# One part of a hybrid encoder step: the gated SSD output kept in its gate's tile, and the Z stores moved to another queue

## The chip, the core and the metric

The program runs on one core of one Trainium2 chip. The metric is the device time of one execution in microseconds. Before the change three runs gave 1900.34, 1905.69 and 1907.13 us; their median is 1905.69 us.

The core has engines with queues of their own that work side by side: TensorE (PE in the profile, its weight loads PEld), VectorE (DVE), ScalarE (ACT), GpSimd (POOL) and SyncE (SP), which here only issues DMAs. An engine takes its instructions in the order of its queue, and an instruction that waits holds up all that stand behind it.

## What is computed

One layer of an encoder runs over 2048 prompt tokens and 64 sample tokens of width 1024, in float32. Cut to what matters here:

```python
h = rmsnorm(x, norm_g)
z_a, xbc, dt_raw, u_b, z_b = split(h @ w_in)
y = ssd_scan(...) + d_ssd[:, None] * xs           # SSD branch, chunk by chunk
y = y * silu(z_a)                                 # its gate
y_a = rmsnorm(y in 4 groups of 256 columns, ssd_norm_g)
y = gelu(S5 scan of u_b); y = y * sigmoid(y @ w_glu + b_glu)
y_b = y * silu(z_b)                               # the gate of the S5 branch
out = rmsnorm(x + concat(y_a, y_b) @ w_out, final_norm_g)
```

The change touches two places: the product `y * silu(z_a)` with its norm, and the store of `silu(z_b)`.

## The kernel before

The tokens are worked through in two stages, `st` 0 (the sample tokens and the first 1024 prompt tokens) and `st` 1 (the other 1024). Within a stage the SSD branch is cut into four groups `g` of four heads. For each group `phase_s_proj` (L746) computes the projections and `phase_s_chunks` (L840) runs the scan, over nine chunks of up to 128 tokens in stage 0 and eight in stage 1. Each matrix product of the projections is done as three matmuls on split halves (`hi`, `lo`) and summed in PSUM.

The gate. `gate()` (L752) projects `z_a` for one chunk after another into a PSUM tile `psz`, and ACT writes `silu(psz)` into a tile `zt` of tag `zs` (L765 to L777). The tag has nine buffers, as many as a group of stage 0 has chunks. The list `zs[c]` keeps them for the scan.

The scan. For each chunk `a1` (L849) transposes inputs on PE into `pA`; `a2` (L867) scales them; `b1` (L888) does the matmuls into `pY` and `pH`; `b2` (L915) updates the state `h` and forms the chunk's output; `b3` (L947) and `b4` (L956) do the norm and the store. The loop at L963 issues `b3`, `b1`, `a1`, then `b4`, `a2`, `b2`, for different chunks. Of the output's path:

```python
act.mul(out=y, in_=pY, mul=ea)                    # b2, L933, four heads
tt(y, y, xs_, ALU.add); tt(y, y, zs[c], ALU.mult) # b2, L935, L936
actf(zs[c], y, AF.Square, accum_out=rs)           # b3, L951, the squares themselves unused
act.mul(out=y, in_=y, mul=rs)                     # b4, L959
pool.dma_start(out=YA[...], in_=y)                # b4, L960
```

The tile `y` (L927) has the pool's two buffers. A buffer is given to the next tile of its tag when all that reads and writes the old one is done, a DMA's landing included; `reuse_waits="tile"` stands at each pool. The PSUM tiles `pA`, `pY`, `pH` and others share the four banks of the pool `sd` (L76); the projections have four banks of their own, the pool `pj` (L75). The norm needs POOL twice: L952 and L953 make the root from the sum `rs`.

The other branch. `phase_uz_block` (L342) projects two blocks of 128 rows of `u_b` or `z_b` into `psu`. ACT copies them (L363) or puts them through Silu (L365) into a tile `ub` (L351) of the pool `big`, seven buffers. POOL then stores U in eight DMAs (L371) or Z in one (L374) per block of 128 rows; there are 16 Z stores in all. Z is read much later, by SP (L1013), into `zt` of `phase_g`.

The order. Generators are woven by hand in the lines from L1306 on: the projections of the S5 branch run as the main thread, with the scan's steps, the preparation of the S5 tables (`PREP`; `prep_mats` L469 and `prep_tabs` L555, mostly on DVE) and in stage 1 the S5 scan (`s5_steps` L663) let in between. That is the order in which the program is written. The builder then sets the order on each engine from a time plan of its own; for ACT and DVE in `phase_g` the written order is kept (`tc.manual_schedule`, L1401 and L1414). In the trace L60 is `tt`, L57 `stt`, L66 `actf`, L69 `mm` and L212 the copy in `split`.

Of the kernel before, what the change touches and what calls it, by code (L numbers as in the profile page):

```python
# [12 lines left out]
AF = mybir.ActivationFunctionType  # L13
ALU = mybir.AluOpType
# [29 lines left out]
def tile_hybrid_stream(  # L44
# [8 lines left out]
    act, dve, pool, sp = nc.scalar, nc.vector, nc.gpsimd, nc.sync  # L53
# [5 lines left out]
    def tt(out, a, b, op):  # L59
        dve.tensor_tensor(out=out, in0=a, in1=b, op=op)  # L60
# [4 lines left out]
    def actf(out, in_, func, **kw):  # L65
        nc.scalar.activation(out=out, in_=in_, func=func, **kw)  # L66
# [12 lines left out]
    Z = dram.tile([8, D, KT], F32, name="Z")  # L79
# [135 lines left out]
    def wblock(segs):  # L215
        his, los = [], []
        n = sum(s[1] for s in segs)
        for kh in range(2):
            raw = rawp.tile([128, 4, 272], F32, tag="raw", name="raw")
            o = 0  # L220
            for c0, w in segs:
                sp.dma_start(out=raw[:, :, o:o + w],
                             in_=w_in[0, kh * 512:(kh + 1) * 512, c0:c0 + w].rearrange("(k p) c -> p k c", p=128))
                o += w
            hi = wp.tile([128, 4, 272], F32R, tag="whi", name="whi")
            lo = wp.tile([128, 4, 272], F32R, tag="wlo", name="wlo")
            split(hi[:, :, :n], lo[:, :, :n], raw[:, :, :n])
            his.append(hi)
            los.append(lo)
        return his, los  # L230

    def proj_cm(ps, W, m0, piece):

        hi, lo, _ = piece
        for k in range(8):
            wh = W[0][k // 4][:, k % 4, m0:m0 + 128]
            wl = W[1][k // 4][:, k % 4, m0:m0 + 128]
            mm(ps, wh, hi[:, k], k == 0, False)
            mm(ps, wh, lo[:, k], False, False)
            mm(ps, wl, hi[:, k], False, k == 7)  # L240
# [95 lines left out]
    def kcols(st):  # L336

        if st == 0:
            return [(0, 0, 64, 0), (0, 64, 256, 9), (1, 0, 384, 41), (2, 0, 384, 89)], 137, 0
        return [(0, 0, 256, 0), (1, 0, 384, 32), (2, 0, 384, 80)], 129, 137  # L340

    def phase_uz_block(st, pcs, blk, kind):  # L342
        runs, K, c0 = kcols(st)
        W = wblock([((C_U if kind == "u" else C_ZB) + 256 * blk, 256)])
        piece_outer = st == 0 and blk == 3 and kind == "z"
        ubs, ths = {}, {}
        order = [(m, i) for i in range(3) for m in range(2)] if piece_outer else [(m, i) for m in range(2) for i in range(3)]
        for m, i in order:
            b = 2 * blk + m
            if i == 0:  # L350
                ubs[m] = big.tile([128, 8, 137], F32, tag="big", name="ub")  # L351
                pool.memset(ubs[m][:, :, 8:9] if st == 0 else ubs[m][:, :, 128:129], 0.0)
            ub = ubs[m]
            ps = pj.tile([128, 512], F32, tag="pj", name="psu")
            proj_cm(ps[:, :PIECES[st][i]], W, 128 * m, pcs[i])
            for (pi, off, n, k0) in runs:
                if pi != i:
                    continue
                nk = n // 8
                src = ps[:, off:off + n].rearrange("p (k s) -> p s k", s=8)  # L360
                dst = ub[:, :, k0:k0 + nk]
                if kind == "u":
                    act.copy(out=dst, in_=src)  # L363
                else:
                    actf(dst, src, AF.Silu)  # L365
            if i < 2:
                yield
                continue
            if kind == "u":
                for j in range(8):  # L370
                    pool.dma_start(out=U[8 * b + j, :, :, c0:c0 + K].rearrange("s c k -> c s k"),  # L371
                                   in_=ub[16 * j:16 * j + 16, :, :K])
            else:
                pool.dma_start(out=Z[:, 128 * b:128 * b + 128, c0:c0 + K].rearrange("s c k -> c s k"), in_=ub[:, :, :K])  # L374
            yield


# [462 lines left out]
    def phase_s_chunks(st, g, p, SS, V):  # L840
# [3 lines left out]
        zs, x0, x1, Bc, Cc = V[g]  # L844

        hsl = slice(4 * g, 4 * g + 4)
        live = {}
# [67 lines left out]
        def b2(c):  # L915

            n, pi, off, cc, ro = chs[c]
            hst, pY, pH, xs_ = live[c]
            sample = st == 0 and c == 0
            zero = st == 0 and c == 1  # L920
            if zero:
                act.copy(out=hst, in_=pH[:, :256])
            else:
                tt(hst.rearrange("p (h q) -> p h q", h=4), hst.rearrange("p (h q) -> p h q", h=4),
                   dec[:, c, hsl].unsqueeze(2).to_broadcast([128, 4, 64]), ALU.mult)
                tt(hst, hst, pH[:, :256], ALU.add)
            y = p.tile([128, 256], F32, tag="y", name="y")  # L927
            tt(xs_[:n], xs_[:n], pY[:n, 0:256], ALU.add)
            if zero:
                tt(y[:n], xs_[:n], zs[c][:n], ALU.mult)  # L930
            else:
                for h in range(4):
                    act.mul(out=y[:n, 64 * h:64 * h + 64], in_=pY[:n, 256 + 64 * h:320 + 64 * h],  # L933
                            mul=ea[:n, c, 4 * g + h:4 * g + h + 1])
                tt(y[:n], y[:n], xs_[:n], ALU.add)  # L935
                tt(y[:n], y[:n], zs[c][:n], ALU.mult)  # L936
            if sample or (c == NC - 1 and st == 1):
                dst = (o_ssd_s if sample else o_ssd_p)[0, 0].rearrange("h p n -> (h p) n")
                pst = sd.tile([128, 512], F32, tag="sd", name="pso")
                for j in range(2):  # L940
                    nc.tensor.transpose(pst[:, 128 * j:128 * j + 128], hst[:, 128 * j:128 * j + 128], ident)
                ho = big.tile([128, 2, 128], F32, tag="big", name="ho")
                act.copy(out=ho, in_=pst[:, :256].rearrange("p (j n) -> p j n", j=2))
                pool.dma_start(out=dst[256 * g:256 * g + 256].rearrange("(j q) n -> q j n", q=128), in_=ho)
            live[c] = y

        def b3(c):  # L947
            n = chs[c][0]
            y = live[c]
            rs = p.tile([128, 1], F32, tag="rs2", name="rs2", bufs=4)  # L950
            actf(zs[c][:n], y[:n], AF.Square, scale=1.0 / 16, accum_out=rs[:n])  # L951
            pool.tensor_scalar(out=rs[:n], in0=rs[:n], scalar1=1.0, scalar2=EPS, op0=ALU.mult, op1=ALU.add)  # L952
            pool.tensor_tensor(out=rs[:n], in0=rs[:n], in1=mhalf[:n], op=ALU.pow)  # L953
            live[c] = y, rs

        def b4(c):  # L956
            n, pi, off, cc, ro = chs[c]
            y, rs = live.pop(c)
            act.mul(out=y[:n], in_=y[:n], mul=rs[:n])  # L959
            pool.dma_start(out=YA[ro:ro + n, 256 * g:256 * g + 256], in_=y[:n])  # L960

# [359 lines left out]
    for b in range(4):  # L1321
        C = phase_s_chunks(0, b, spool, SS, V)
        if b == 0:
            pp = aux.enter_context(tc.tile_pool(name="pp", bufs=1, reuse_waits="tile"))
            P = []
            PP = prep_params(pp, P)
            weave(phase_uz_block(0, pcs, 0, "u"), (PP, 1.34), (C, RA))
            drain(PP)
            pw = aux.enter_context(tc.tile_pool(name="pw", bufs=1, reuse_waits="tile"))
            PREP = chain(*(chain(prep_mats(k, pw, P), prep_tabs(k, 0, pw, P), prep_tabs(k, 1, pw, P)) for k in range(4)))  # L1330
            weave(phase_uz_block(0, pcs, 0, "z"), (C, RA), (PREP, RP))
            drain(C)
            weave(phase_s_proj(0, pcs, 1, spool, SS, V), (PREP, RP))
        elif b < 3:
            weave(chain(phase_uz_block(0, pcs, b, "u"), phase_uz_block(0, pcs, b, "z")), (C, RA), (PREP, RP))
            drain(C)
            weave(phase_s_proj(0, pcs, b + 1, spool, SS, V), (PREP, RP))
        else:
            weave(phase_uz_block(0, pcs, 3, "u"), (C, RC), (PREP, RP))
            drain(PREP)  # L1340
# [110 lines left out]
```

## Time and profile before

| | |
|---|---|
| three runs, median | 1905.69 us (1900.34 to 1907.13) |
| the profiled execution, its own time | 1902.07 us |
| its span, from the first instruction to the last | 1900.3 us |
| mean granted clock of TensorE | 0.989 |
| busy: PE, PEld, DVE, ACT, POOL | 1831.1, 1709.4, 1096.5, 908.6, 378.3 us |
| DMA, mean rate over the span | 129 GB/s |

The scans and projections take the time to about 1366 us, with the work of `phase_g` from 1290 to 1507 us and the output projection after that. How to read the rows below: in a list of waits a line is the engine and source line that waited, what ended the wait, the total in us, the number of times and the longest. In a timeline a line is start, duration, engine, source line, operation, the tile written and the tiles read, the shapes, and a count of merged instructions; in brackets stands how long the engine sat idle before it and what ended that. An engine with a q behind it (ACTq) is its queue, seen at issuing a DMA.

### The profile page before, as it was taken

The page shows a single profiled execution, that of the slowest core. Times are in us where ns is not written, and L with a number is a line of the kernel's source. Part 1 is how long each engine was busy: PE and PEld are TensorE (multiplying, and loading weights), DVE is VectorE, ACT ScalarE, POOL GpSimd, SP SyncE. Part 2 cuts the span into 40 slices and gives each one's busy share as a digit, 9 for nine tenths or more (in the row PEclk, how much of TensorE's full clock was granted, in tenths as well). Part 3 has the DMA queues.
Part 4 walks back from the last instruction along what each step waited for, and adds up shares of the span by engine and source line. Part 5 has one row for each costly group of instructions (what it writes and reads, how often), then busy time and mean ns, then how long its engine had stood idle before and what let it go on. Part 6 is the DMA issues. An engine that isn't in the chain of part 4 may idle for free. (4 is left out here: it accounts for less than half of the span.)

```text
span 1900.3 us, 31061 instructions
## 1 busy us (share of the span) xinstructions
PE 1831.1 (96%) x11400; PEld 1709.4 (90%) x11400; DVE 1096.5 (58%) x2157; ACT 908.6 (48%) x2505; POOL 378.3 (20%) x730
## 2 busy tenths in 40 slices
PE   7998999999899899999999999999999999999998
PEld 6998999999899799889989999998999988887886
DVE  5688687685767653776678567857544432212221
ACT  5466465545646633666666556656544421111110
POOL 3022314233332411032013301212211000001000
PEclk9999999999999999999999999999999999999999
DMA  5224545454444454456545754536455553313220
GB/s 165 76 72 101 155 105 137 127 137 103 121 128 111 143 137 119 139 153 182 152 136 164 206 159 125 152 95 178 134 161 161 186 181 92 97 56 95 92 86 34
DMA packets 197816, 244.69 MB, mean 129 GB/s; under 512 B 41696, under 2 KB 158432, under 8 KB 197664
## 3 DMA queue, kind: packets, MB, share of 16 engines
q1 hardware_dynamic: 170944, 167.49, 31.7%
q0 software_dynamic: 25136, 74.66, 13.4%
q8 instruction: 90, 1.47, 0.3%
q10 hardware_dynamic: 1584, 0.56, 0.2%
q14 instruction: 62, 0.51, 0.1%
HBM read 171.09 MB, written 75.75 MB: 130 GB/s over the span
## 5 line engine op out<-in xcount | busy, mean ns | idle before, releaser
L69 PE MATMUL psp<-whi,yy 128*128 128x512 f32 x1056 | 333.6, 394 | 1.3 <-ACT yy L212 1.3
L69 PE MATMUL psu<-hh,whi 128*128 128x384 f32 (+2 forms) x768 | 259.1, 337 | 0.8 <-DVE hl L60 0.8
L69 PE MATMUL psr<-hh,whi 128*128 128x384 f32 (+2 forms) x768 | 256.8, 335 | 3.1 <-ACT whi L212 3.1
L69 PE MATMUL psr<-hh,wlo 128*128 128x384 f32 (+2 forms) x768 | 249.4, 325 | 1.8 <-DVE wlo L60 1.8
L69 PE MATMUL psu<-hl,whi 128*128 128x384 f32 (+2 forms) x768 | 250.3, 326 | 0.0
L69 PE MATMUL psu<-hh,wlo 128*128 128x384 f32 (+2 forms) x768 | 250.1, 326 | 0.0
L69 PE MATMUL psr<-hl,whi 128*128 128x384 f32 (+2 forms) x768 | 249.9, 325 | 0.0
L69 PEld LDWEIGHTS psp<-whi,yy 128*128 128x128 f32 x1056 | 198.2, 188 | 48.9 <-ACT yy L212 1.5
L69 PE MATMUL psp<-wlo,yy 128*128 128x512 f32 (+1 forms) x544 | 214.8, 395 | 0.0
L69 PE MATMUL psz<-whi,hh 128*128 128x256 f32 (+1 forms) x512 | 151.4, 296 | 0.4 <-DVE dtr L60 0.4
L69 PEld LDWEIGHTS psr<-hh,whi 128*128 128x128 f32 x768 | 146.1, 190 | 4.5 <-ACT whi L212 3.3
L69 PE MATMUL psz<-whi,hl 128*128 128x256 f32 (+1 forms) x512 | 147.0, 287 | 1.4 <-DVE hl L60 1.4
L69 PEld LDWEIGHTS psr<-hh,wlo 128*128 128x128 f32 x768 | 145.7, 190 | 2.5 <-DVE wlo L60 2.3
L69 PEld LDWEIGHTS psu<-hh,whi 128*128 128x128 f32 x768 | 145.4, 189 | 2.1 <-DVE hl L60 1.0
L69 PEld LDWEIGHTS psr<-hl,whi 128*128 128x128 f32 x768 | 146.0, 190 | 1.2
L69 PE MATMUL psz<-wlo,hh 128*128 128x256 f32 (+1 forms) x512 | 147.0, 287 | 0.0
L69 PE MATMUL psg<-gh,glo 128*128 128x266 f32 x512 | 146.1, 288 | 0.9 <-DVE glo L60 0.9
L69 PE MATMUL psg<-gl,ghi 128*128 128x266 f32 x512 | 146.6, 289 | 0.0
L69 PEld LDWEIGHTS psu<-hl,whi 128*128 128x128 f32 x768 | 145.5, 189 | 1.1
L69 PEld LDWEIGHTS psu<-hh,wlo 128*128 128x128 f32 x768 | 145.3, 189 | 0.3
L69 PE MATMUL psg<-gh,ghi 128*128 128x266 f32 x512 | 144.0, 288 | 0.0
L60 DVE TENSOR_TENSOR wlo<-raw,whi 128x1024 fp32r<-128x1024 f32 (+1 forms) x80 | 97.9, 1225 | 78.9 <-ACT whi L212 77.3
(559 smaller groups left out, 3914.6 us busy)
## 6 DMA issues: line engine op xcount, KB each, us to landing
raw<-in_w_in_dram SPq DMA_DIRECT2D x64, 512.0 KB
tab<-TAB SPq DMA_DIRECT2D x64, 266.0 KB
xt<-in_x_prompt_dram SPq DMA_DIRECT2D x32, 512.0 KB
abc<-atd SPq DMA_DIRECT2D x64, 256.0 KB
TAB<-k POOLq DMA_DIRECT2D x32, 266.0 KB, 3.7
ut<-U SPq DMA_DIRECT2D x32, 266.0 KB
Y<-bs POOLq DMA_DIRECT2D x32, 266.0 KB, 3.8
G<-Y SPq DMA_DIRECT2D x128, 66.5 KB
```

The costliest lines, as they stand in the source:

```text
L60: dve.tensor_tensor(out=out, in0=a, in1=b, op=op)
L69: nc.tensor.matmul(out, lhsT=lhsT, rhs=rhs, start=start, stop=stop)
```

## The change

The chunk's gated product is written into the tile of its gate, `zs[c]`, instead of `y`. The Square reads `zs[c]` and writes its unused squares into `y`. The scaling by `rs` works in place on `zs[c]`, and the store to YA reads it from there. For the one chunk with no earlier state (`zero`) `y` is then written by the Square alone. Apart from that, the Z stores are issued from ACT's queue instead of POOL's.

```diff
@@ phase_uz_block
             else:
-                pool.dma_start(out=Z[:, 128 * b:128 * b + 128, c0:c0 + K].rearrange("s c k -> c s k"), in_=ub[:, :, :K])
+                act.dma_start(out=Z[:, 128 * b:128 * b + 128, c0:c0 + K].rearrange("s c k -> c s k"), in_=ub[:, :, :K])
             yield
@@ phase_s_chunks, b2
             if zero:
-                tt(y[:n], xs_[:n], zs[c][:n], ALU.mult)
+                tt(zs[c][:n], xs_[:n], zs[c][:n], ALU.mult)
             else:
...
                 tt(y[:n], y[:n], xs_[:n], ALU.add)
-                tt(y[:n], y[:n], zs[c][:n], ALU.mult)
+                tt(zs[c][:n], y[:n], zs[c][:n], ALU.mult)
@@ phase_s_chunks, b3
-            actf(zs[c][:n], y[:n], AF.Square, scale=1.0 / 16, accum_out=rs[:n])
+            actf(y[:n], zs[c][:n], AF.Square, scale=1.0 / 16, accum_out=rs[:n])
@@ phase_s_chunks, b4
-            y, rs = live.pop(c)
+            y, rs = zs[c], live.pop(c)[1]
             act.mul(out=y[:n], in_=y[:n], mul=rs[:n])
             pool.dma_start(out=YA[ro:ro + n, 256 * g:256 * g + 256], in_=y[:n])
```

## Rows read from the trace of the kernel before

**Rows 1.** The page: busy us, share of the span and instructions of each engine.

```profile
PE 1831.1 (96%) x11400; PEld 1709.4 (90%) x11400; DVE 1096.5 (58%) x2157; ACT 908.6 (48%) x2505; POOL 378.3 (20%) x730
```

**Rows 2.** Waits of PE, whole span: us in total, times, longest us.

```profile
PE pY L69 <- DVE E L60: 9.2, 11, 2.1
PE pA L856 <- ACT y L933: 4.6, 2, 3.8
...
PE psb L537 <- ACT y L933: 1.3, 1, 1.3
```

**Rows 3.** Waits of DVE and ACT, whole span.

```profile
DVE y L60 <- ACT y L933: 49.2, 29, 11.3
...
ACT y L933 <- DMA YA<-y: 10.5, 5, 4.9
```

**Rows 4.** Timeline of POOL, 484 to 488 us.

```profile
484.64 0.96 POOL L374 DMA_DIRECT2D Z<-ub  x1
...
486.55 0.93 POOL L374 DMA_DIRECT2D Z<-ub  x1 [0.27 <-POOL R L696]
487.48 0.56 POOL L960 DMA_DIRECT2D YA<-y  x1
```

**Rows 5.** Timelines of ACT and PE, 496 to 498 us.

```profile
496.43 0.93 ACT L933 ACTIVATE y<-pY,ea 128x64 f32<-128x64 f32 x4 [4.86 <-DMA YA<-y]
...
497.41 0.47 PE L856 MATMUL pA<-ident,cv 128*128 128x128 f32 x1 [3.77 <-ACT y L933]
```

**Rows 6.** The stores of tile YA, all 68: from issue to landing.

```profile
DMA to landing us min/median/max: 1.9/3.0/9.3
```

**Rows 7.** Stretches: length, busy us of PE, PEld, DVE, ACT, POOL, granted clock, DMA.

```profile
390.00:394.00 4.00, 4.00 (x20) 4.00 (x20) 4.00 (x4) 2.71 (x6) 0.85 (x1) 0.57 0.25 63
496.00:503.00 7.00, 5.59 (x27) 5.59 (x28) 5.38 (x23) 5.53 (x24) 1.36 (x3) 0.51 0.09 14
```

**Rows 8.** Timelines of ACT and PE, 321 to 324 us.

```profile
321.75 1.75 ACT L933 ACTIVATE y<-pY,ea 128x64 f32<-128x64 f32 x8 [1.23 <-DMA YA<-y]
...
322.74 0.66 PE L537 MATMUL psb<-ident,k 128*128 128x128 f32 x4 [1.25 <-ACT y L933]
```

**Rows 9.** Timelines of ACT, DVE and PE, 642 to 649 us.

```profile
642.57 1.75 ACT L933 ACTIVATE y<-pY,ea 128x64 f32<-128x64 f32 x8 [3.42 <-DMA YA<-y]
...
643.53 0.43 DVE L60 TENSOR_TENSOR y<-y,xs__7180 128x256 f32<-128x256 f32 x1 [3.91 <-ACT y L933]
...
647.40 1.10 PE L69 MATMUL pY<-xd,E 128*128 128x64 f32 x8 [1.46 <-DVE E L60]
```

**Rows 10.** Timelines of DVE at 361 us and of PE at 388 us.

```profile
360.78 0.43 DVE L60 TENSOR_TENSOR y<-y,xs__3937 128x256 f32<-128x256 f32 x1 [11.29 <-ACT y L933]
...
388.36 1.97 PE L69 MATMUL pk<-s,k 128*128 128x16 f32 x16 [2.16 <-DVE k L60]
```

**Rows 11.** Tile Z: ns min/median/max of an issue, first and last; then ACT's queue, timeline.

```profile
L374 POOL DMA_DIRECT2D Z<-ub x16: 885/920/979, 162.8 to 1198.3; - x16
...
47.06 0.67 ACTq L392 DMA_DIRECT2D KP<-zz  x1
...
103.83 1.46 ACTq L398 DMA_DIRECT2D prow<-in_lam_im_dram  x1
```

**Rows 12.** Timeline of ACT, 727 to 730 us: the first instruction after a block's last Silu.

```profile
729.58 0.39 ACT L66 ACTIVATE ub<-psu 128x256 f32<-128x256 f32 x1 [2.35 <-PE psu L69]
```

**Rows 13.** Timeline of PE, 163 us.

```profile
163.14 1.10 PE L69 MATMUL pY<-xd,E 128*128 128x64 f32 x8 [0.63 <-DVE E L60]
```

**Rows 14.** Timelines of ACT and POOL, 362 to 367 us.

```profile
362.82 0.41 ACT L66 ACTIVATE zs<-y 128x256 f32<-128x256 f32 x1
...
363.35 0.39 ACT L66 ACTIVATE zs<-psz 128x256 f32<-128x256 f32 x1
...
366.40 0.59 POOL L960 DMA_DIRECT2D YA<-y  x1 [0.85 <-ACT k L564]
```

## The prediction

> **What bounds the kernel now.** I began with the totals by engine. TensorE (PE) is busy for 1831.1 of 1900.3 us, ScalarE (ACT) for 908.6 and GpSimd (POOL) for 378.3 [rows 1]. So only about 69 us can be won by better order, however much work leaves ACT or POOL, and a change that removes no matmul is worth what it takes out of PE's idle time. The next view is PE's waits by what ended them, and there the reader should look for the lines of the diff [rows 2]. Two of the waits end on ACT's `y` of L933, the scaling that fills the tile `y` in `b2`: 4.6 us ahead of the transposes of L856 and 1.3 us ahead of those of L537. None of the waits listed for PE ends on POOL. Then I asked what ACT's L933 itself waits for [rows 3]: five times, 10.5 us in all, it waits for the store of YA to land, since `y` has two buffers and the store reads `y`. Behind ACT stands VectorE (DVE): it waited 29 times, 49.2 us, for this same `y`.
>
> The timeline shows the largest case. POOL issues two Z stores at 484.64 and 486.55 and one YA store behind them at 487.48 [rows 4]. The next L933 can begin only at 496.43, after 4.86 us in which ACT waited for that store [rows 5], so 8.9 us after its issue, where the median of a YA store is 3.0 us [rows 6]. PE stood for 3.77 us until L933 had read `pY` and so freed its bank for the next `pA` [rows 5]. The granted clock then was 0.51 over 496 to 503 us, in effect the lower of the two levels, 1.2 GHz, after PE had stood idle [rows 7].
>
> **The change, part by part.** The gated product is now made in `zs[c]`, and the square that sums for the norm puts its unneeded result into `y`. The final scaling and the store use `zs[c]`. No instruction is added or removed here and every shape stays, so the work itself costs nothing. What moves is who holds a buffer. `y` is free when the Square of its chunk is done, on the same engine that writes it next, so the wait for YA is gone. `zs` (nine buffers) is held until the store lands, so the first instruction queued behind such a store is the Silu of a later gate tile.
>
> (a) The stall at 493: 3.77 us of idle PE, and in the 5.59 us that PE was then busy at a clock of 0.51 it lost 5.59 x 0.49 = 2.7 us [rows 5, 7]. Together 6.5 us. ACT had nothing else to do in its 4.86 us, so L933 can start before PE asks for the bank. Ends: 3.0 (half comes back as another wait) to 6.5. I take 6.5, as the whole wait has one releaser.
>
> (b) At 321.75 ACT waited 1.23 us for YA, and PE stood 1.25 us behind it [rows 8]. Ends 0 and 1.25; I take 1.25, since the two waits end within a microsecond of each other.
>
> (c) At 642.57 ACT waited 3.42 us, so DVE stood 3.91 us, and its queue then was late with the `E` that ends PE's 1.46 us at 647.40 [rows 9]. Ends 0 and 2.9 (twice the row, for smaller waits around it). I take 1.46.
>
> (d) A late consequence. DVE stood 11.29 us until 360.78 for L933, which ACT had been given only behind the Silus of the next gate, and the tables and matrices that DVE also prepares stood behind it in its queue. At 388.36 PE waited 2.16 us for such a matrix (`pk`), and the clock from 390 to 394 was 0.57, a loss of 4.00 x 0.43 = 1.7 us [rows 7, 10]. The order on each engine is written by the builder from a time plan in which `y` waits for a store; without that wait L933 can stand earlier. Ends 0 and 3.9. I take 3.9, because DVE's 11.29 us are five times what PE lacked.
>
> (e) The 16 Z stores leave POOL, 0.92 us each, 14.7 us in all [rows 11]. I cost this at nothing gained on PE, for no wait of PE ends there, and count only that YA no longer stands behind Z. Past POOL's queue the stores go to ACT's, where each needs ACT's last Silu finished and holds ACT's sequencer. The trace has no Z store there. The nearest row is ACT's own store to KP, which by the code has 1,024 pieces, as many as a Z store: 0.67 us [rows 11]. Ends: 0 where ACT would have waited anyway, as after 727 us, when its next instruction had stood idle for 2.35 us [rows 12]; and 1.46, the longest issue on ACT's queue [rows 11]. What ACT loses reaches PE only where PE has no slack. PE stood for a short while within 4 us of a Z issue at three places, near 163, 1028 and 1200 us; the first is shown, 0.63 us [rows 13]. I take 3 x 0.67 = 2.0 us. The other 13 are covered by ACT's idle half [rows 1] and by the four banks of the projections; without that cover they would cost 13 x 0.67 = 8.7 us more.
>
> The two issues on ACT's queue, 0.67 and 1.46 us, differ by more than two times [rows 11]. The Trainium skill (Perfetto Trace Analysis, section "DMA Instruction — HWDGE (DVE, Sync)") says that two sequencers share the block that makes descriptors, and that one which issues first waits for its lock. By that rule SP's loads would lengthen ACT's issues: (e) would be 3 x 1.46 = 4.4 us and the sum 8.6 us. Of 16 new issues no row here can show it; it is what the rival "ACT pays" below turns on.
>
> (f) The builder's order can change anywhere, with no row to price it. I bound it by the pattern most common in PE's waits, 9.2 us in 11 waits for `E` [rows 2]: 9.2 either way, taken as 0.
>
> **Sum:** 6.5 + 1.25 + 1.46 + 3.9 - 2.0 = 11.1 us less. The profiled execution had 1902.07 us (its span 1900.3 and 1.8 around it), so it would be 1891.0. The median of the three runs shown, 1905.69, lies 3.6 us above it, and the forecast is made from the median: 1894.6 us, or 0.58% less. About 0.5%, here 9.5 us, is what a measurement of this kernel can tell from no change; the runs shown span 6.8 us.
>
> **Rivals.**
> *The stall moves.* L933 starts earlier, but the plan puts something else in its place, and (c) and (d) give nothing. For it: DVE's and PE's orders are planned anew, and PE waits 11 times for `E` now. Against: (a) and (b) have one direct releaser, which goes. Time: 1905.7 - 6.5 - 1.25 + 2.0 = 1900.0 us, within 0.5%.
> *The wait goes to `zs`.* At 363.35 the last gate Silu of a group takes a tile right after the Square of 363 us freed it; the YA store of that chunk is issued at 366.40 [rows 14] and would land 3.0 us later [rows 6], so this Silu would wait 6.0 us, with ACT's copies of the next projection behind it and PE behind those. For it: nine chunks use all nine buffers. Against: it falls only at the end of a group, and the chunk's tail itself should come earlier. If it all reached PE, with a loss of clock as in (a), 6.0 + 2.7: 1894.6 + 8.7 = 1903.3 us.
> *ACT pays.* Each Z issue keeps ACT from copies that PE waits for: 16 x 1.46 = 23.4 us, with only (a) kept: 1905.7 + 23.4 - 6.5 = 1922.6 us, slower. For it: ACT issues in order, and the store must wait for ACT's own Silu. Against: ACT is idle for half its time and PE lists no long wait for a projection's bank. With all my gains it breaks even at 13.1/16 = 0.82 us per store, and it decides for slower by 0.5% from 1.4 us per store that reach PE.
>
> **How the numbers follow.** Chances: forecast 0.50, the stall moves 0.26, the wait goes to `zs` 0.13, ACT pays 0.11. Of the forecast, 0.03 falls short of 9.5 us. So faster 0.47, within 0.5% 0.42, slower 0.11. Low end: all gains at their upper ends (6.5 + 1.25 + 2.9 + 3.9 = 14.6), no cost, and half of (f): 1905.7 - 14.6 - 4.6 = 1886.5. High end: the `zs` rival with half of (f), 1903.3 + 4.6 = 1907.9. That leaves out "ACT pays" and a little on each side.
>
> **What would show it.** Right: no wait of L933 for a DMA; no PE idle of over 1 us before L856 or L537 with ACT's `y` as releaser; DVE's 49.2 us for L933 down by a third or more; 16 issues on ACT's queue near 0.67 us; POOL busy for 14 us less. Wrong: new waits of ACT's gate Silu for a YA store; PE idle before projections whose releaser is ACT just after a Z issue; or PE's idle total near 69 us with new places. If PE's idle falls by 10 us or more and the time does not, my reading that idle is what counts is wrong.

## The result, and the profile after

Beside runs of the kernel before (median of four 1904.22 us, 1900.34 to 1907.13), four runs of the changed kernel gave a median of 1888.13 us (1883.32 to 1891.88). The ratio is 0.9919, 95% interval [0.9901, 0.9937]: faster by 0.8%. On a second chip it was 0.9891 [0.9876, 0.9906] (below). The forecast was 1894.6 us in a range of 1886.5 to 1907.9. The profiled execution took 1885.5 us with a span of 1883.7, 16.6 us shorter than the span before.

The totals by engine on the page of the changed kernel:

```profile
PE 1824.1 (97%) x11400; PEld 1706.5 (91%) x11400; DVE 1099.4 (58%) x2157; ACT 909.2 (48%) x2505; POOL 364.3 (19%) x714
```

Against [rows 1] POOL is busy for 14.0 us less and issues 16 instructions less. PE is busy for 7.0 us less with the same 11,400 matmuls, and idle for 1883.7 - 1824.1 = 59.6 us in place of 69.2. The two make the 16.6 us. The busy time fell with the mean granted clock, 0.992 in place of 0.989, for the work is the same.

The waits of PE and DVE in the changed kernel, whole span (us in total, times, longest):

```profile
PE pY L69 <- DVE E L60: 7.1, 6, 2.3
...
PE psc L508 <- ACT cn L505: 3.3, 1, 3.3
...
PE pA L856 <- ACT y L933: 1.5, 1, 1.5
```

```profile
DVE y L60 <- ACT y L933: 32.1, 35, 4.1
```

DVE's 49.2 us for L933 [rows 3] are down by 35%. ACT's list has no wait of L933 for a store of YA any more, and the wait of `psb` for L933 [rows 2] is gone. The largest new size is the wait for `cn`, the sign change of a table input (L505). It is one wait, for the last of four such sign changes, and the kernel before has it too, shorter and at 519.27 us:

```profile
PE psc L508 <- ACT cn L505: 1.4, 1, 1.4
```

In the changed kernel it falls near the time of the stall of [rows 5]. The timelines of ACT and PE:

```profile
489.04 1.07 ACT L582 ACTIVATE k<-k,sm__1136 128x64 f32<-128x64 f32 x4
...
492.14 1.27 ACT L586 ACTIVATE k<-k,cm 128x128 f32<-128x128 f32 x4
...
493.57 0.40 ACT L505 ACTIVATE cn<-cn 128x256 f32<-128x256 f32 x1
...
494.03 0.69 PE L508 MATMUL psc<-ident,cn 128*128 128x128 f32 x2 [3.26 <-ACT cn L505]
```

ACT does not wait here, it works: 4.4 us of table work (L582, L586), from 489.04 to 493.41, stand ahead of `cn` in its queue.

One sign of being right did not come: PE still stands for over 1 us before L856 with ACT's `y` as releaser (the line of 1.5 us above, at 149.53). The kernel before has 0.87 us there, and at that place no L933 waits for a store in either kernel, so the hold is not the reason.

To see where the time went, the same work must be compared. Both kernels run the 3,904 matmuls into `psu` and `psz` in the same order, so I cut the span at the start of number 324, 972, 1296, 1782, 2106 and 3888. Five stretches, first of the kernel before, then of the changed kernel (length, busy us of PE, PEld, DVE, ACT, POOL, granted clock, share of the time that the 16 DMA engines are busy, where 1 is full, and GB/s):

```profile
128.30:331.70 203.40, 196.22 (x1293) 189.38 (x1292) 159.00 (x375) 114.54 (x387) 70.10 (x123) 0.98 0.47 121
331.70:440.70 109.00, 106.79 (x725) 104.48 (x723) 80.02 (x211) 58.92 (x180) 33.02 (x60) 0.98 0.49 126
440.70:593.60 152.90, 146.24 (x949) 143.13 (x949) 94.16 (x243) 77.11 (x244) 42.42 (x79) 0.97 0.44 113
593.60:684.00 90.40, 80.05 (x533) 75.09 (x532) 60.15 (x120) 61.89 (x206) 34.87 (x72) 0.98 0.51 143
684.00:1292.40 608.40, 593.06 (x3786) 568.63 (x3785) 411.10 (x695) 358.36 (x972) 112.63 (x230) 0.99 0.53 146
```

```profile
127.70:326.20 198.50, 193.25 (x1295) 187.21 (x1294) 160.22 (x388) 116.77 (x397) 67.72 (x124) 1.00 0.50 125
326.20:431.30 105.10, 105.10 (x724) 102.84 (x722) 78.33 (x197) 57.78 (x173) 29.43 (x56) 1.00 0.51 130
431.30:583.00 151.70, 146.47 (x967) 143.51 (x966) 101.96 (x261) 82.66 (x267) 43.45 (x81) 0.98 0.45 116
583.00:667.00 84.00, 77.64 (x517) 75.22 (x516) 54.85 (x102) 56.73 (x184) 32.03 (x66) 0.96 0.49 150
667.00:1275.40 608.40, 591.88 (x3786) 567.55 (x3785) 412.07 (x695) 358.05 (x972) 106.32 (x222) 0.99 0.53 146
```

The gains are 4.9, 3.9, 1.2, 6.4 and 0.0 us, 16.4 in all, and all of it falls in stage 0. The stretch that holds the stall near 493 gave only 1.2. Two things belong to these numbers.

The third and the fourth stretch are the same work only together. The 17 matmuls of one chunk (into `pY`, `pH` and `pA`) run in the fourth in the kernel before, from 594.91 to 597.24, and in the third in the changed kernel, from 578.58 to 580.91. PE's timelines show where they start:

```profile
594.91 0.68 PE L69 MATMUL pY<-xd,E 64*64 64x64 f32 x8
```

```profile
578.58 0.67 PE L69 MATMUL pY<-xd,E 64*64 64x64 f32 x8
```

They take 2.33 us in either. So for equal work the third stretch gave 3.5 us and the fourth 4.1.

The first stretch differs between two executions of the changed kernel itself: 198.5 us here, 203.2 in run 4 below, with the same idle of PE (5.2 us). Here the granted clock stayed up behind the stalls, there it fell. Ten us of each:

```profile
178.00:188.00 10.00, 10.00 (x81) 9.90 (x80) 8.19 (x14) 6.25 (x20) 3.26 (x5) 1.00 0.51 148
```

```profile
178.00:188.00 10.00, 10.00 (x50) 9.90 (x50) 6.60 (x11) 3.40 (x10) 1.54 (x2) 0.62 0.26 69
```

In the kernel before it is 0.67 from 148 to 158 us. That is some 3 of the 4.9 us, and they are not shown to be the change's; the other 2 are idle time of PE.

### The profile page after: what moved, and what is told of

It reads as the page before. It is cut to its first block, busy times and chain, and to the rows that moved or that the text cites. A ratio compares the mean times of both kernels' runs of the same rounds, so it can differ in the third digit from the quotient of the medians.

```text
span 1883.7 us, 31097 instructions
## 1 busy us (share of the span) xinstructions
PE 1824.1 (97%) x11400; PEld 1706.5 (91%) x11400; DVE 1099.4 (58%) x2157; ACT 909.2 (48%) x2505; POOL 364.3 (19%) x714
## 4 chain that ended last, share of the span: by engine, by line
PE 72%; DVE 11%; ACT 7%; DMA 4%; issue 3%; POOL 1%; ACTq 0%; SPq 0%; DVEq 0%; POOLq 0%
PE psp L69 20%; PE psr L69 14%; PE psu L69 12%; PE psg L69 9%; PE psz L69 7%; PE pY L69 2%; PE psy L69 2%; DMA xt<-in_x_prompt_dram 2%; DVE cv L57 2%; DVE E L861 1%; ACT y L933 1%; DVE b L60 1%; PE psi L69 1%; PE pH L69 1%; PE pso L1146 1%
```

## The experiments

There were four groups of runs, each on one chip with runs of the kernel before beside it; ratios are to those. The median of the kernel before was 1909.11, 1909.80, 1910.89 and 1908.82 us.

**1. The tile part alone.** The changed kernel with the one line of L374 put back.

```diff
-                act.dma_start(out=Z[...], in_=ub[:, :, :K])
+                pool.dma_start(out=Z[...], in_=ub[:, :, :K])
```

> The change with the Z stores left on GpSimd: only the product is made, scaled and stored in the tile of its gate. Theory (the wait of L933 for the store of YA is what cost): no L933 waits for a DMA, DVE's wait for y falls from 49.2 to about 32 us, PE's idle falls by 8 to 10 us, and the time is 12 to 16 us under the kernel before (ratio 0.9915 to 0.9940). Rival 1 (moving the Z stores carries the gain): within 4 us of the kernel before. Rival 2 (any new plan of the builder is worth up to 9 us either way): the time is under the kernel before but over 5 us away from the changed kernel.

Measured: 1896.33 us, 0.9932 [0.9918, 0.9945], 12.8 us under the kernel before. No L933 waits for a DMA, and DVE waits 31.6 us for `y`. The tile part carries most of the gain. But PE's stall near 490 is larger than before, 7.06 us, and it is for `cn`. The timelines of POOL, SP's queue, ACT and PE in this kernel, and then the stretch from 486 to 492 us, here and in the kernel before:

```profile
481.90 0.97 POOL L374 DMA_DIRECT2D Z<-ub  x1
482.86 2.17 POOL L960 DMA_DIRECT2D YA<-zs  x4
...
486.96 1.37 SPq L501 DMA_DIRECT2D cn<-in_c_im_dram  x1
...
496.05 0.42 ACT L505 ACTIVATE cn<-cn 128x256 f32<-128x256 f32 x1 [7.07 <-DMA cn<-in_c_im_dram]
...
496.52 0.69 PE L508 MATMUL psc<-ident,cn 128*128 128x128 f32 x2 [7.06 <-ACT cn L505]
```

```profile
486.00:492.00 6.00, 3.46 (x30) 3.25 (x28) 3.71 (x20) 2.45 (x8) 2.08 (x5) 1.00 1.04 195
```

```profile
486.00:492.00 6.00, 5.63 (x43) 5.22 (x42) 5.15 (x21) 3.87 (x15) 3.18 (x8) 1.00 1.06 232
```

The load of `cn` was issued at 486.96, into a stretch in which the DMA engines were busy without a pause (share 1.04), and landed 9 us later. In the kernel before they were as full there (1.06), and the transfer that somebody waited for then was the store of YA. So the wait for YA went, and the next late transfer of the same few microseconds took its place.

**2. The Z part alone.** The kernel before with L374 on `act`.

> The other part alone: the Z stores go to ScalarE's queue, y stays as before. Theory: the YA store of the chunk near 487 us no longer stands behind two Z stores, so its landing falls from 9.3 us to about 3 and the 3.77 us of idle PE near 493 with its 2.7 us of clock go or shrink, while the other four waits of L933 (about 5.6 us) stay; 16 issues of 0.37 us on ACT cost 0 to 2 us; the time is 2 to 7 us under the kernel before (ratio 0.9963 to 0.9990). Rival 1 (the tile carries all): within 2 us of the kernel before. Rival 2 (the move of Z carries most): 10 us or more under it. Rival 3 (ACT pays): 2 us or more over it.

Measured: 1909.05 us, 0.9997 [0.9988, 1.0007]: nothing. Rival 1 holds by the time. What the theory said of its one place did happen: no L933 waits for YA between 321 and 628 us, and the YA stores beside a Z store there, issued at 479.21 and 488.16, land after 4.2 and 3.9 us, where the one of [rows 4] took 8.9. (The 9.3 us of the expectation are those of another store, at 1049 us.) So POOL's queue had a part in that stall. But over the whole span YA lands no sooner (median 3.3 us, longest 9.0, against 3.0 and 9.3 in [rows 6]), and L933 waits for it six times, 15.3 us in all, the longest 5.14 us at 628.72. For this one the stores were issued at 622.4 and 622.9 with no Z store in the 12 us before, and the share of the DMA engines was 0.97 to 1.04 from 624 to 632 us. PE's stall for `cn` is there too, 3.63 us at 517.76.

**3. The store alone moved to the gate's tile.** The kernel before, with the product and the Square as they were.

```diff
-            act.mul(out=y[:n], in_=y[:n], mul=rs[:n])
-            pool.dma_start(out=YA[...], in_=y[:n])
+            act.mul(out=zs[c][:n], in_=y[:n], mul=rs[:n])
+            pool.dma_start(out=YA[...], in_=zs[c][:n])
```

> The kernel before with one edit: the scaling by rs in b4 reads y and writes zs, and the store to YA reads zs. y then is free when that scaling is done and no store holds it, but it is held longer than in the changed kernel, where the Square frees it some us earlier. Z stays on GpSimd. Theory (the landing of the store is the whole wait): as the tile part alone, 12 to 16 us under the kernel before, and no L933 waits for a DMA. Rival (the earlier release by the Square is what counts): under half of that, 0 to 6 us, with L933 or DVE waiting for y about as long as before (49.2 us).

Measured: 1895.61 us, 0.9924 [0.9912, 0.9936], as the tile part alone. No L933 waits for a DMA, and DVE waits 21.7 us for `y`. That the Square frees `y` some microseconds earlier adds nothing that can be told.

**4. The changed kernel again,** on the chip of experiments 5, 7 and 8.

> The changed kernel once more, beside the kernel before on the chip of the three runs that follow, as the mark for them. Expected by every theory: 14 to 18 us under the kernel before (ratio 0.9905 to 0.9925).

Measured: 1888.84 us, 0.9891 [0.9876, 0.9906].

**5. The hold put back** (the hold: the store keeps `y` until it has landed). The complement of 3: product and Square in the gate's tile, Z on ACT, but the store leaves from `y`.

```diff
-            y, rs = zs[c], live.pop(c)[1]
-            act.mul(out=y[:n], in_=y[:n], mul=rs[:n])
+            y, rs = live.pop(c)
+            act.mul(out=y[:n], in_=zs[c][:n], mul=rs[:n])
```

> The changed kernel with one edit back: the scaling by rs reads zs and writes y, and the store to YA leaves from y. The product and its Square stay in the tile of the gate, and Z stays on ScalarE; only the hold of y by the store is back. Theory (that hold is the whole cost): the gain goes, the time is within 4 us of the kernel before (ratio 0.998 to 1.002), and L933 waits for YA for about 10 us again. Rival (the product in zs, or merely another plan of the builder, carries it): within 4 us of the changed kernel (ratio 0.990 to 0.994).

Measured: 1908.19 us, 0.9992 [0.9981, 1.0002]: the whole gain is gone. Where, show the stretches between the same matmuls, first of run 4, then of this kernel:

```profile
128.10:331.30 203.20, 197.98 (x1294) 191.79 (x1293) 160.08 (x387) 116.31 (x395) 67.23 (x124) 0.97 0.50 122
331.30:436.40 105.10, 105.10 (x724) 102.85 (x722) 78.55 (x199) 57.62 (x173) 29.75 (x56) 1.00 0.52 130
436.40:588.90 152.50, 146.79 (x967) 143.63 (x966) 101.97 (x261) 82.75 (x267) 43.47 (x81) 0.98 0.46 115
588.90:672.60 83.70, 77.75 (x516) 75.15 (x515) 54.80 (x102) 56.67 (x183) 31.97 (x66) 0.96 0.51 151
```

```profile
126.80:330.90 204.10, 196.61 (x1294) 189.56 (x1294) 159.15 (x378) 115.66 (x391) 66.27 (x122) 0.98 0.50 122
330.90:441.80 110.90, 108.42 (x724) 106.02 (x722) 80.26 (x207) 58.97 (x178) 29.95 (x57) 0.97 0.48 123
441.80:594.50 152.70, 146.14 (x967) 142.09 (x967) 98.57 (x258) 80.77 (x263) 46.31 (x81) 0.99 0.45 114
594.50:686.80 92.30, 79.82 (x515) 74.69 (x515) 56.29 (x105) 58.25 (x188) 30.76 (x66) 0.96 0.48 137
```

The hold costs 0.9, 5.8, 0.2 and 8.6 us. These stretches hold the same matmuls in both kernels (28 into `psz`, within the third, stand in another order). In the third no L933 waits for a store here, as in experiment 2, and PE's stall for `cn` is 3.6 us with the hold against 3.4 without. How the hold reaches PE in the last stretch, three rows of its timelines of ACT, DVE and PE show:

```profile
621.96 1.83 ACT L933 ACTIVATE y<-pY,ea 128x64 f32<-128x64 f32 x8 [5.14 <-DMA YA<-y]
...
622.92 0.42 DVE L60 TENSOR_TENSOR y<-y,xs__7030 128x256 f32<-128x256 f32 x1 [8.81 <-ACT y L933]
...
626.24 1.08 PE L69 MATMUL pY<-xd,E 128*128 128x64 f32 x8 [3.31 <-DVE E L60]
```

ACT waits for the store, DVE for ACT, and the `E` that stands behind `y` in DVE's queue comes late to PE.

**6. Z on SyncE.** The changed kernel with L374 on `sp`.

> The changed kernel with the Z stores issued by SyncE instead of ScalarE. It takes 16 issues of 0.37 us, 5.9 us in all, off ACT's queue, and puts a wait for ACT's Silu into the queue that issues the loads of weights and inputs. Theory (ACT's issues are covered by its idle half; in the trace of the changed kernel one of them, at 1006.62 us, is followed by 0.9 us more idle PE): within 2 us of the changed kernel. Rival 1 (ACT pays for them on the path): 4 to 6 us under the changed kernel. Rival 2 (a load stands behind a Z store in SP's queue): 4 us or more over the changed kernel, with PE waiting for a weight tile.

Measured, on the chip of experiments 1 to 3: 1893.33 us, 0.9913 [0.9900, 0.9926], between the two ratios of the changed kernel. No cost of ACT's issues can be told. The 0.9 us that I had put down to the issue near 1007 us is no cost of it: in experiment 1, where POOL issues Z, the same wait of `psy` lasts 1.63 us too.

**7. `cn` on GpSimd.** The sign changes of L503 and L505 as `pool.tensor_scalar`, to take that stall out of ACT's queue.

> The changed kernel with the eight sign changes of cn (L503, L505) made by GpSimd instead of ScalarE. In the changed kernel PE stood 3.26 us near 491 for one of them, which stood in ACT's queue behind 4.5 us of table work and a gate Silu, and lost 1.7 us of clock after it. Theory (that stall took the place of the one which the change removed, and it is one of ACT's order): the stall goes and the time is 2 to 5 us under the changed kernel. Rival 1 (something else is late at that place, the table k of DVE): within 2 us of the changed kernel, with another releaser near 491. Rival 2 (the GpSimd passes, longer than ACT's 0.4 us, hold up the norm's small operations there): 2 us or more over it.

Measured: 1890.70 us, 0.9902 [0.9886, 0.9917], no gain over run 4. The timelines of POOL and PE in this kernel at that place:

```profile
496.24 0.61 POOL L960 DMA_DIRECT2D YA<-zs  x1 [0.84 <-ACT zs L959]
496.89 0.42 POOL L505 TENSOR_SCALAR cn<-cn 128x256 f32<-128x256 f32 x1
...
497.36 0.44 PE L508 MATMUL psc<-ident,cn 128*128 128x128 f32 x2 [2.29 <-POOL cn L505]
```

The wait is shorter and still there, only with another releaser: now the sign change stands in POOL's queue behind a YA store that itself waited for ACT. Rival 1 holds by the time, though not with the releaser that it named.

**8. Z stored twice by ScalarE,** to price an issue: a second DMA of the same tile into a spare tensor `Z2`, right behind L374.

> The changed kernel with every Z store issued twice by ScalarE, the second into a spare tensor: 16 more issues of about 0.37 us, 5.9 us in all, on ACT's queue. Theory (ACT's idle half covers them, at most 3 of 16 reach PE): 0 to 2 us over the changed kernel. Rival 1 (ACT pays for all): 5 to 9 us over it. Rival 2 (issues block each other's descriptors, up to the 1.46 us of the longest issue seen): issues of 0.7 us and more, and over 10 us over the changed kernel.

Measured: 1920.24 us, 1.0048 [1.0033, 1.0064], 31 us over run 4. Rival 2 alone allowed that much, but by issues of 0.7 us and more; the second ones took 0.61 at the median. Two views of this kernel, in which the lines below L79 stand one or two later: first the issues of the tile Z (ns min/median/max), then waits of SP, PE and DVE (us in total, times, longest):

```profile
L375 ACTq DMA_DIRECT2D Z<-ub x16: 366/366/385, 161.2 to 1216.3; - x16
L376 ACTq DMA_DIRECT2D Z<-ub x16: 454/606/1885, 161.7 to 1216.7; - x16
```

```profile
SPq L611 <- DMA Z<-ub: 7.5, 2, 6.1
SPq L608 <- DMA Z<-ub: 4.4, 1, 4.4
SPq L609 <- DMA Z<-ub: 2.9, 1, 2.9
...
PE psi L69 <- DMA ut<-U: 4.9, 1, 4.9
...
DVE E L863 <- DMA abc<-atd: 14.0, 2, 13.2
```

The 16 added issues are 16 x 0.61 = 9.7 us of ACT's queue, but PE's waits for ACT are 8.0 us in all, less than the 12.6 of run 4; those for DVE and DMAs rose from 39.8 to 62.0 us. New are waits for loads: `ut`, an input of the S5 scan, and 14.0 us for `abc`, an input of the chunks (3.8 in the changed kernel). SP's loads of `tab`, `ut` and `bl`, all for the S5 scan, also stood 14.8 us for the landing of a Z store with which they share no data. In the trace the DMAs of SP and ACT carry the same eight completion semaphores, and those of POOL eight others, which made this a suspect of its own. The next three runs ask whether it is the pieces, the semaphores or the bytes.

**9. Z by rows.** The changed kernel with one tensor for each stage, laid out so that a row of `ub` is one run.

```diff
-    Z = dram.tile([8, D, KT], F32, name="Z")
+    Z01 = [dram.tile([D, 8, k], F32, name=f"Z{i}") for i, k in enumerate((137, 129))]
...
-                act.dma_start(out=Z[...], in_=ub[:, :, :K])
+                act.dma_start(out=Z01[st][128 * b:128 * b + 128], in_=ub[:, :, :K])
...
-        sp.dma_start(out=zs[q], in_=Z[t, 256 * q:256 * q + 256]...)
+        for s_, k0, k1 in ((0, 0, 137), (1, 137, 266)):
+            sp.dma_start(out=zs[q][:, :, k0:k1], in_=Z01[s_][256 * q:256 * q + 256, t]...)
```

> The changed kernel with Z laid out by rows, one tensor for each stage, so that a Z store writes 128 runs of 4,384 or 4,128 bytes in place of 1,024 runs of 548 or 516; the bytes are the same. Each read of Z in the gate of the S5 branch becomes two DMAs (64 in place of 32, on SyncE). Doubling the stores had cost 31 us, 1.96 us for each, while ACT's issues came to 0.37 and 0.61 us. Theory (a store of 1,024 pieces keeps the DMA engines from the other transfers, and pieces are what counts): transfers issued within 7 us of a Z store land sooner (YA now 4.6 us there at the median against 2.5 elsewhere), and the time is 5 to 20 us under the changed kernel (ratio to the kernel before 0.979 to 0.988). Rival 1 (one store of Z is hidden where two are not): within 4 us of the changed kernel. Rival 2 (the split reads pay): 4 us or more over it, with the loss after 1290 us.

Measured: 1886.02 us, 0.9875 [0.9857, 0.9893]. This is the lowest ratio of all, and it lies below the kernel before by 1.25%. From run 4 (0.9891) it can't be told apart, so rival 1 holds.

**10. The second copy by rows.** Experiment 8 with the copy laid out as in 9: the same bytes, an eighth of the pieces.

> The changed kernel with its Z stores as they are, and a second copy of the same tile stored behind each into a spare tensor by rows, 128 runs of 4,384 or 4,128 bytes. It adds as many bytes and as many issues by ScalarE as the run with Z stored twice did, but an eighth of the pieces. Theory (the number of pieces cost the 31 us): 0 to 6 us over the changed kernel. Rival 1 (bytes, or the longer hold of ub): 12 to 30 us over it. Rival 2 (the new plan of the builder alone cost it): any value, with PE's stalls at places where no load is late.

Measured: 1919.36 us, 1.0045 [1.0031, 1.0060], as dear as 8. The number of pieces is not the cost.

**11. The second copy on GpSimd.** Experiment 8 with `pool.dma_start` for `Z2`.

> The changed kernel with its Z stores on ScalarE as they are, and the second copy of each into the spare tensor issued by GpSimd. Bytes and pieces are those of the run with Z stored twice by ScalarE, which cost 31 us. In that run SyncE's loads stood up to 6.1 us, 14.8 us in four waits, for the landing of a Z store that they have nothing to do with. Theory (what cost there is that ScalarE's and SyncE's transfers share completion semaphores, so that a load stands behind a Z store that landed late): SyncE has no wait for Z, and the time is 2 to 12 us over the changed kernel (ratio to the kernel before 0.991 to 0.997). Rival (the bytes cost: twice as much in the DMA engines beside the loads, or ub held longer): 20 to 35 us over it (1.000 to 1.009) without any such wait.

Measured: 1921.68 us, 1.0063 [1.0050, 1.0076], as dear again, although SP's waits for Z have shrunk to two of 2.6 and 2.2 us. So it is not ACT's queue, and the semaphores are at most a small part. Nor is it one plan of the builder: of the 3,904 matmuls into `psu` and `psz`, 104 stand at other places than in the changed kernel in experiments 8 and 10, and none in experiment 11. What the three have in common are the bytes, one more store of 561 or 528 KB beside each. One stretch of 20 us around the same Z store, in run 4 and then here:

```profile
864.00:884.00 20.00, 19.38 (x146) 18.44 (x145) 10.43 (x17) 12.72 (x33) 2.95 (x7) 1.00 0.93 234
```

```profile
888.00:908.00 20.00, 14.54 (x111) 13.70 (x108) 8.18 (x12) 9.66 (x25) 3.81 (x7) 0.96 1.06 229
```

With one Z store the DMA engines have a share of 0.93 there and PE is busy for 19.4 of 20 us. With two they are full, they move no more in a second (229 against 234 GB/s), and PE has 4.8 us less. That the longer hold of `ub` adds to it was not separated.

**12. Z by rows on GpSimd.** Experiment 9 with `pool` for the store.

> The kernel with Z by rows in long runs, its Z stores back on GpSimd, so the queue move of the change undone in that layout. Theory (the queue of a single Z store hardly counts): within 3 us of the layout by rows on ScalarE (ratio to the kernel before 0.986 to 0.989). Rival (a Z store on GpSimd holds the YA stores behind it, whose landing beside a Z store was 6.9 us at the median with the tile part alone and 4.6 us in the changed kernel): 3 to 8 us slower than on ScalarE (0.989 to 0.992).

Measured: 1895.45 us, 0.9934 [0.9920, 0.9948], against 0.9875 on ACT: 0.6% or 11 us slower, and the intervals don't meet. The rival holds in its direction, and the loss is larger than it said. Its reason is not shown: the YA stores within 7 us after a Z store land after 4.6 us at the median against 4.0 in experiment 9, and no L933 and no gate's Silu waits for one in either. Each of the two kernels has its own plan, too. In the old layout the same step is 0.9932 (experiment 1) against 0.9919, where the intervals overlap, and 0.9891, where they don't. In experiment 2, with the hold in place, the queue of Z is worth nothing.

## Why the prediction was right, and where not

The forecast (faster, 0.5) came true, with 11.1 us said and 16.1 measured. Its main reason is shown from both sides: the release of `y` from the store is enough for the gain (experiment 3), and the hold alone is enough to lose it (experiment 5). Nine kernels, each with its own plan from the builder, fall into two groups with a gap between them: those with the hold at 0.9997 and 0.9992, those without it and with each Z stored once at 0.9875 to 0.9934. The terms by which I came to it did worse than the sum: for equal work (a) was 3.0 us too large, (c) 2.6 too small and the 2.0 of (e) were not lost. These errors offset each other, so that the sum came this near is in part luck.

**(a), the stall near 493, 6.5 us: wrong.** "I take 6.5, as the whole wait has one releaser" is the step that failed. The wait went, but for equal work its stretch gave 3.5 us. PE stands there for other things instead: for `cn` 3.26 us in place of 1.44, for `pk` 1.98 in place of 0.75, and a slow clock comes behind these too (0.50 from 494 to 497 us). The releaser was one transfer among several that were late in the same full stretch of the DMA engines; with the tile part alone PE then waited 7.06 us for the load of `cn`, and in the changed kernel 3.26 us for ACT. Here the rival "the stall moves" came true for its reason, though not in its terms: it kept (a) and gave up (c) and (d). Experiment 5 says nothing of (a), as no L933 waits for a store in that stretch there. I had read [rows 4] as a store behind two others in POOL's queue, which experiment 2 bears out for this one stall, and had not looked at the DMA share of that stretch.

**(b), 1.25 us: not contradicted.** The wait at 321.75 is gone, and with the hold back PE stands there for 2.24 us. PE's idle in the first stretch fell from 7.2 to 5.2 us, in both profiles of the changed kernel. Besides the wait at 321.75 that is a shorter one near 175, 1.14 us in place of 2.20, of which I had said nothing.

**(c), 1.46 us with a bound of 2.9: right mechanism, size too small.** For equal work it measured 4.1 us, and 8.6 in experiment 5. The chain by `E` is the one that I named, but it recurs: with the hold back, the waits of L933 for YA are 15.8 us, and one of them alone keeps PE for 3.31 us. I had summed PE's waits with a direct row and left out what a late DVE does to the later ones. PE's wait for `xt` (L322), 4.49 us in the kernel before and 2.01 in the changed kernel, may be one of these; that was not separated.

**(d), 3.9 us: right size, reason not shown.** The stretch gave 3.9 us, and 5.8 in experiment 5; the wait for `pk` and its slow clock are gone. But DVE still stands there as long, now for ACT's split of a weight:

```profile
355.68 1.23 DVE L60 TENSOR_TENSOR wlo<-raw,whi 128x1024 fp32r<-128x1024 f32 x1 [12.48 <-ACT whi L212]
```

So a DVE that stands for 11.29 us [rows 10] does not by itself make `pk` late. All three kernels with the hold have this wait for `pk`, 2.0 to 2.2 us near 388 to 404, and no other kernel has more than 0.3 us of it there, so it belongs to the hold; by what way is open.

**(e), 2.0 us lost: wrong in sign.** The tile Z in the changed kernel (issues, ns min/median/max):

```profile
L374 ACTq DMA_DIRECT2D Z<-ub x16: 366/366/413, 160.2 to 1182.1; - x16
```

An issue took 0.37 us where I had 0.67, 5.9 us in all. No cost of it on PE can be told (experiment 6). Once `y` is free, Z on ACT rather than on POOL gains: 0.13 and 0.41% by the two ratios of the changed kernel against experiment 1, of which the first is within the noise, and 0.6% by experiments 9 and 12. By the rule of the Trainium skill (Perfetto Trace Analysis, section "DMA Instruction — HWDGE (DVE, Sync)") on the lock of the block that makes descriptors, (e) would have been 4.4 us (and the sum 8.7, not 8.6). Single stores here, 0.41 us at most, show no such wait; the second of two in a row took 0.61 us at the median and up to 1.9 (experiment 8).

**(f), taken as 0:** stage 1 has the same length to 0.1 us, so the builder's freedom cost and gave nothing there. In stage 0 it can't be told from (a) to (d).

Of the other rivals, "the wait goes to `zs`" left no sign: no gate's Silu waits for a store in the changed kernel (experiment 3 has one such wait, of 3.0 us). "ACT pays" is refuted at 0.37 us an issue.

## What to carry to other kernels

Before a wait for a transfer is counted as won, look at the DMA share of that stretch: where the engines are full, the next transfer that somebody needs can be late too, and the stall changes its name. A buffer that a fast loop reuses should not be the source of a store; let the last operation write to a buffer whose next user is far away. Where the order is made from a plan, compare stretches between the same numbered matmuls, count what else runs in them, and look at the granted clock of each; single stalls wander.

## What the hardware showed unexpectedly

- **A large store delays the others from whichever queue.** YA stores issued within 7 us after a Z store landed after 5.3 us at the median before the change and 5.0 with Z on ACT (experiment 2), against 2.8 and 3.1 us elsewhere (up to 1250 us). Once `y` is free they are 6.9 with Z on POOL (experiment 1) and 4.0 and 4.6 with Z on ACT (the two profiles of the changed kernel), so more behind a Z store in the same queue. With Z stored twice the median there was 8.2 to 11.9 us. The Trainium skill (DMA: Bandwidth & Descriptors, section "Issuing engines are not separate DMA queues") says that DMAs of the scalar, sync and gpsimd engines run on the same 16 DMA engines and interleave. These runs agree with that. It also says that another issuing engine saves issuing time only; experiments 9 and 12, 11 us apart for 16 issues of 0.45 or 0.73 us, say that the queue, with the plan that the builder makes for it, can matter more.
- **One more store of 561 or 528 KB beside each of 16 cost 2 us of the kernel each**, whether in 1,024 pieces or 128, on ACT or on POOL, though the share of the DMA engines over the whole span is only about half. Whether the longer hold of `ub` has a part in it is open.
- **A load can stand for a foreign store:** up to 6.1 us in experiment 8, where loads on SP's queue waited for Z stores of ACT's queue to land. With each Z stored once no such wait is listed.
